# Attention's values by seven products, split between the recurrence and the projections, with ten pairs' first sums kept in DRAM

## The chip, the cores and the metric

The kernel runs on one core of one Trainium2 chip. That core has TensorE (PE in the profile; its weight loads are PEld), VectorE (DVE), ScalarE (ACT), GpSimd (POOL) and SyncE (SP, which issues most transfers). The metric is the device time in microseconds of one execution, and the time of a kernel is the median of its runs.

## The reference

One layer of an encoder on x of 1024 positions by 1024 features, all in float32. An input projection gives attention's q, k and v, the q, k, v and output gate of a gated linear attention (GLA), its decays, and two merge gates; then

```python
proj = x @ w_in[l]
(aq, ak, av, gq, gk, gv, gout, lr_f, lr_b, gate_a, gate_g) = jnp.split(proj, IN_SPLITS, axis=-1)
# mixer A: 12 heads of 64 in three groups (window, dilation) = (128,1), (512,4), (2048,16):
#   softmax over a dilated window with a position bias, o_g and its denominator per group
y_attn = jnp.sum(mix_w[..., None] * jnp.stack(outs, axis=0), axis=0)      # 4 heads x 64
# mixer B: chunked recurrence over chunks of 64, forward and backward, 4 heads
o_gla = o_fwd + o_bwd
y_gla = o_gla * lax.rsqrt(mean(o_gla**2) + eps) * gla_norm_g * silu(gout)
merged = sigmoid(gate_a) * (y_attn @ w_attn_branch) + sigmoid(gate_g) * (y_gla @ w_gla_branch)
x = _layernorm(ALPHA * x + merged @ w_out, ...)
x = _layernorm(ALPHA * x + square(relu(x @ w_ff1 + b_ff1)) @ w_ff2 + b_ff2, ...)
```

Attention's values `av`, which the change is about, are x (1024 x 1024) times a weight of 1024 x 768.

## The kernel before

**Arithmetic.** TensorE multiplies in a format of fewer bits than float32. Each operand is therefore split in two: a hi part, rounded by a cast on ACT, and a lo part, the operand less its hi part, by a subtraction on DVE (`halve`, `load_w`, `fm_pairs`). `mm3` makes each product as three matmuls: hi by hi (L102), hi by lo (L103), lo by hi (L104). The three lines carry nearly all matmuls of the kernel.

**Seven products.** A product of two matrices, each cut in 2 x 2 blocks, can be made of seven block products instead of eight, of sums of blocks (the Strassen-Winograd form). The kernel calls them m1 to m7, or M1 to M7. Their sides are A11, S1, S2, A12, S3, A22, S4 from the weights and B11, B21, T1 to T4, B22 from x. The T sums of x are made by `xsum` on DVE (L497) and split into `xT1` to `xT4`. A partial result that several blocks share (`cu`, the u2 of the form) is kept in SBUF; `cr` holds a result before SP stores it to the DRAM tensor `spill`.

**The order of the work.** The kernel is written in the order in which the engines get their work; each engine has its own queue and runs it in order, and `tc.issue_after` places an instruction behind a named earlier one in the scheduler's order. The stages are:

1. Start: the first blocks of GLA's q and k, then the decays and the values of GLA's first group (to 78.8 us, with the first heads' gating).
2. The recurrence (78.8 to 210.6 us). Each of four heads goes through `pre1`, `pre2`, `turn`, `intra`, `kv`, `states`, `out`, `outt`. Between these small steps stand big independent matmul units, the `fills`, taken by `fill(n)`: 8 units of GLA's values, 4 of its q and k, and 16 units of attention's V. A V unit is a token tile of 128 rows by 384 columns over all eight k-blocks, 24 matmuls, whose result ACT copies to `stgv` (L470) and SP stores to the DRAM tensor `vdr`. `extra` names for each fill by its number (`count`) what is done after it: loads and splits of later weights. Behind the last head's `out` the rest of the fills, three V units, stand ahead of `outt`.
3. The feature-major projections, in pairs of 128-row blocks (`proj`), by seven products, each of 12 matmuls of 512 columns (four k-blocks by three parts). The first two pairs (blocks 4 to 7, the GLA output gate) have M1 and M2 made together ahead of a list `steps`, which holds a preparation (a side) and a product each. Then come 14 pairs of seven steps: the q and k blocks of attention's groups 2, 1, 0 and eight pairs of merge gates.
4. Attention: 24 tiles (`att`), handled in 26 visits (`visit(i)`). A visit is a unit that runs ahead of a step, every 2.5 steps before the change: scores on PE, bias and maximum on DVE (L828), exponent on ACT (L834), transposes and the product with V in later visits. The loop over `steps` runs at step i the units named for i, then the preparation of step i + 3, and then the products of step i. The GLA output gating (`silu`, L979 and L980 on DVE) is among the units too.
5. Branches and merge, w_out, LayerNorm, the two feed-forward products (seven products each), LayerNorm. The change does not touch them.

TensorE's results go to PSUM tiles `mm`, `sc`, `tr`; `p_raw` (4 buffers) holds raw weights, `p_side` (7 buffers, named pwhi, pwlo, px after their pools) the split sides, and `p_sum` (psum) the running sum.

## Time and profile before

| | |
|---|---|
| median of 3 runs (lowest, highest) | 1370.29 us (1369.72, 1371.16) |
| the profiled execution's own time | 1370.95 us |
| its span, first to last instruction | 1368.5 us |
| mean granted TensorE clock | 0.998 |
| busy PE / PEld / DVE / ACT / POOL | 1357.7 / 1130.7 / 1008.9 / 630.5 / 113.6 us |
| moved by DMA | 241.75 MB, 177 GB/s on average |

All lines below are of one profiled execution. Busy time counts an engine's instructions without double counting of overlaps; matmuls overlap in the records, so a busy PE tells that something was in the pipeline, and the distance between starts tells how fast it ran. A row of windows gives, for one stretch of time, the busy microseconds of each engine with the number of its instructions in brackets, then the granted clock, the DMA share and the rate. A row of waits names the waiting instruction, an arrow, the instruction that released it, and the total, the number and the longest of the waits. A row of groups gives the line, the operation, output and inputs with their shape and count, the total and mean (ns) of one, and the idle time ahead of them on that engine with its cause.

### The profile page before, as it was taken

What the parts mean: (1) busy time and instruction counts of PE and PEld (TensorE: products, weight loads), DVE (VectorE), ACT (ScalarE), POOL (GpSimd) and SP (SyncE); (2) the same over time, 40 slices, a digit from 0 to 9 for tenths busy, and PEclk for the clock granted to TensorE, in tenths of its full rate; (3) what the DMA queues carried; (4) which work ended last, traced back from release to release, by engine and by line L of the source; (5) the groups of instructions that cost most, each with busy time, mean ns of one, the idle gap of its engine ahead of it and who ended that gap; (6) DMA issues with size and microseconds to landing.
All of it is one profiled execution on the core that took longest, in us unless ns stands there. A gap on an engine that the chain in (4) does not pass through costs nothing.

```text
span 1368.5 us, 18991 instructions
## 1 busy us (share of the span) xinstructions
PE 1357.7 (99%) x6829; PEld 1130.7 (83%) x6829; DVE 1008.9 (74%) x1748; ACT 630.5 (46%) x1207; POOL 113.6 (8%) x173
## 2 busy tenths in 40 slices
PE   9999999999999999999999999999999999999998
PEld 7989998877778777788888888888888888888886
DVE  7377767776566688767667778877867897786988
ACT  5346645334344444455326655555556433333343
POOL 0000100013333333100001000000000000000002
PEclk9999999999999999999999999999999999999999
DMA  8262326664554577665935465666645954445313
GB/s 254 67 200 80 104 75 193 207 189 142 162 172 140 154 214 173 202 229 194 339 127 197 160 223 199 215 206 211 244 178 176 372 204 156 154 142 162 97 31 123
DMA packets 119234, 241.75 MB, mean 177 GB/s; under 512 B 33269, under 2 KB 42133, under 8 KB 119140
## 3 DMA queue, kind: packets, MB, share of 16 engines
q1 hardware_dynamic: 111764, 220.57, 48.7%
q0 software_dynamic: 6944, 19.54, 5.0%
q8 instruction: 53, 0.87, 0.3%
q10 hardware_dynamic: 432, 0.44, 0.1%
q14 instruction: 41, 0.34, 0.1%
HBM read 163.81 MB, written 77.73 MB: 177 GB/s over the span
## 4 chain that ended last, share of the span: by engine, by line
PE 88%; DVE 5%; DMA 3%; ACT 2%; issue 1%; POOL 0%; SPq 0%; ACTq 0%; DVEq 0%; POOLq 0%
PE ps L102 18%; PE ps L103 18%; PE ps L104 18%; PE mm L102 8%; PE mm L103 8%; PE mm L104 8%; PE sc L822 1%; PE avp L861 1%; PE tr L846 1%; DMA pwhi<-in_wfm 1%; DVE cr L654 1%; ACT xr L1261 1%; PE sc L409 0%; DMA xr<-in_xT 0%; PE tr L379 0%
## 5 line engine op out<-in xcount | busy, mean ns | idle before, releaser
L1242 ACT CAST T<-hp 128x1024 fp32r<-128x1024 f32 x36 | 37.9, 1052 | 110.7 <-PE ps L103 71.0
L103 PE MATMUL mm<-wlo,x 128*128 128x272 f32 (+1 forms) x240 | 74.5, 311 | 0.7 <-DVE wlo L95 0.7
L102 PE MATMUL mm<-whi,x 128*128 128x272 f32 (+1 forms) x240 | 75.0, 313 | 0.0
L104 PE MATMUL mm<-whi,x 128*128 128x272 f32 (+1 forms) x240 | 74.7, 311 | 0.0
L103 PE MATMUL ps<-B,B 128*128 128x512 f32 x160 | 62.2, 389 | 0.0
L104 PE MATMUL ps<-B,B 128*128 128x512 f32 x160 | 62.2, 389 | 0.0
L102 PE MATMUL ps<-B,B 128*128 128x512 f32 x160 | 60.9, 390 | 0.5 <-ACT B L1242 0.5
L1748 POOL TENSOR_TENSOR mv<-mv,mhalf 128x1 f32<-128x1 f32 x8 | 7.0, 880 | 607.3 <-DVE mv L1747 605.8
L834 ACT ACTIVATE e<-e,sm 128x256 f32<-128x256 f32 (+2 forms) x96 | 43.4, 453 | 30.0 <-DVE sm L828 29.9
L102 PE MATMUL ps<-T,T 128*128 128x512 f32 x144 | 56.0, 389 | 0.0
L103 PE MATMUL ps<-T,T 128*128 128x512 f32 x144 | 56.0, 389 | 0.0
L104 PE MATMUL ps<-T,T 128*128 128x512 f32 x144 | 56.0, 389 | 0.0
L102 PE MATMUL ps<-B,T 128*128 128x512 f32 x144 | 56.0, 389 | 0.0
L103 PE MATMUL ps<-B,T 128*128 128x512 f32 x144 | 56.0, 389 | 0.0
L104 PE MATMUL ps<-B,T 128*128 128x512 f32 x144 | 56.0, 389 | 0.0
L1243 DVE TENSOR_TENSOR T<-hp,T 128x1024 fp32r<-128x1024 f32 x36 | 43.9, 1221 | 15.5 <-ACT T L1242 15.4
L1643 DVE TENSOR_TENSOR acc<-ps,acc 128x512 f32<-128x512 f32 x68 | 45.5, 685 | 12.8 <-PE ps L104 12.3
L102 PE MATMUL mm<-x,pwlo 128*128 128x512 f32 x128 | 50.7, 396 | 0.7 <-ACT cu L659 0.7
L654 DVE TENSOR_TENSOR cr<-cu,mm 128x512 f32<-128x512 f32 x44 | 35.2, 800 | 20.3 <-PE mm L104 20.1
L102 PE MATMUL ps<-T,fraw 128*128 128x512 f32 x128 | 49.6, 390 | 0.4 <-ACT T L1242 0.4
L104 PE MATMUL mm<-x,pwlo 128*128 128x512 f32 x128 | 49.9, 390 | 0.0
L103 PE MATMUL mm<-x,pwlo 128*128 128x512 f32 x128 | 49.9, 389 | 0.0
(492 smaller groups left out, 4197.2 us busy)
## 6 DMA issues: line engine op xcount, KB each, us to landing
hdr<-c SPq DMA_DIRECT2D x112, 256.0 KB, 3.0
hp<-hdr SPq DMA_DIRECT2D x56, 512.0 KB, 3.9
spill<-cr SPq DMA_DIRECT2D x64, 256.0 KB, 2.9
praw<-in_wfm SPq DMA_DIRECT2D x16, 512.0 KB, 5.3
pwhi<-in_wfm SPq DMA_DIRECT2D x16, 512.0 KB, 4.6
gate<-spill SPq DMA_DIRECT2D x32, 256.0 KB, 3.1
wa<-in_w SPq DMA_DIRECT2D x16, 512.0 KB, 4.4
wb<-in_w SPq DMA_DIRECT2D x16, 512.0 KB, 7.2
```

Source lines behind the costliest of these rows:

```text
L102: T.matmul(ps, lh, rh, start=first and i == 0, stop=False, skip_group_check=more)
L103: T.matmul(ps, lh, rl, start=False, stop=False, skip_group_check=more)
L104: issued["pe"] = T.matmul(ps, ll, rh, start=False, stop=last and i == n - 1, skip_group_check=more)
L654: issued["add"] = V.tensor_tensor(o, a, b, op=OP.add)
L822: mm = T.matmul(sps[i][:, pr, 0:w], q[ps_, pr], k[ps_, pr, 0:w], start=True, stop=True)
L834: issued["exp"] = A.activation(e, e, AF.Exp, bias=sm[:, h:h + 1], scale=-1.0, accum_out=sm[:, 4 + h:5 + h])
L846: T.transpose(tp[0:hi - lo, pr, j], b["e"][i][:, pr, lo:hi], ident)
L861: return T.matmul(av[64 * i:64 * i + 64, pr], vv[:, h * 64:h * 64 + 64], b["et"][i][p0:p0 + vv.shape[0], pr, j], start=j == pr == 0, stop= ...
L1242: A.copy(o[:, 0], src)
L1243: V.tensor_tensor(o[:, 1], src, o[:, 0].bitcast(F32), op=OP.subtract)
L1261: A.activation(q[i][:, k], tp[:, k], AF.Identity, bias=cols[:, c + 8:c + 9], scale=cols[:, c:c + 1])
L1643: V.tensor_tensor(m, p, m, op=OP.add)
```

## The change

V is made by seven products too. Its 1024 x 768 weight is cut into 2 x 2 blocks of 512 x 384, x likewise. M1 and M2 of V are made for four token tiles in the recurrence (`att_v`, `part`): M1's sum is stored in a DRAM tensor `vpk`, M1 + M2 in `vdr`. The other five products of V are ten half-steps (`v_prep`, `v_do`, with two of the four k-blocks each) in `steps`, behind the first two pairs and ahead of the rest. `v_fetch` loads raw V weights into `p_raw`, `v_kept` reads `vpk` back into attention's R tiles `vu`, and the sums go into attention's av and ak tiles `vx`.

Ten of the 14 later pairs (`KEPT`) make M1 and M2 in the recurrence as well (`first_two`): raw weights are loaded and split, M1 is copied by ACT and stored to a DRAM tensor `upk`, and M1 + M2 to `spill`. Their `proj` then has five steps in place of seven; the first of them (`sums`) reads `upk` back into `cu` and prepares S1 and S2. The fills of the recurrence become 12 + 14 in place of 28; each of the 14 (`two`) holds two half units of 12 matmuls each, of 512 columns for a pair and 384 for V, in the order of `halves`, so that M1 of the next stands between M1 and M2 of one. One fill in place of three stands behind the last head's `out`.

The list `steps` has 98 entries in place of 108, visits come at fixed steps (`at`), and the gating units come earlier in time beside the V half-steps, in other buffers. The core of the diff:

```diff
-    def att_v(c):
-        w, raws, order = {}, [], (0, 1, 2, 3) if c == 0 else (3, 0, 1, 2)
+    todo = [((4, 5), 1), ((6, 7), 1)]
+    for g in (2, 1, 0):
+        todo += [((b + 2 * g, b + 2 * g + 1), ORD[g]) for b in (24, 30)]
+    todo += [((b, b + 1), 1) for b in range(8, 24, 2)]
+    NP = len(todo)
+    KEPT = 10
+
+    def after_raw(f, *a):
+        with tc.issue_after(issued["raw"].ins):
+            return f(*a)
+
+    def keep(dst, ps, r=1):
+        n = ps.shape[1]
+        o = xb_t() if n == 512 else stg.tile([128, n], F32, tag="stgv", bufs=2, name="stgv")
+        o = o.rearrange("p (c j) -> p c j", c=r)
+        A.copy(o, ps.rearrange("p (j c) -> p c j", c=r))
+        SP.dma_start(dst, o if r > 1 else o[:, 0])
+
+    def first_two(p):
+        (b0, _), r = todo[2 + p]
+        st = {}
+
+        def fetch_raw():
+            st["raw"] = wp.tile([128, KT, 128], F32, tag="raw", bufs=2, name="raw")
+            issued["raw"] = after_raw(SP.dma_start, st["raw"], io["wfm"][b0])
+
+        def split():
+            st["w"] = fm_pairs(*load_w(None, [128, KT, 128], st["raw"]), 0)
+
+        def m1():
+            st["ps"] = mmtile()
+            mm3(st["ps"], st["w"][0:4])
+            keep(upk[p], st["ps"])
+
+        def m2():
+            mm3(st["ps"], st["w"][4:8], False, True, True)
+            keep(spill[b0].rearrange("p (c h j) -> p h c j", h=2, c=r)[:, 0] if r > 1 else spill[b0][:, 0:512], st["ps"], r)
+        return fetch_raw, split, m1, m2
+
+    def att_v():
...
+        def part(t, h):
             ts = slice(t * 128, t * 128 + 128)
-            mm3(ps, [(xh(k, ts), xl(k, ts), w[k // 2][0][:, k % 2], w[k // 2][1][:, k % 2])
-                     for i in order for k in (2 * i, 2 * i + 1)])
-            o = stg.tile([128, 384], F32, tag="stgv", bufs=2, name="stgv")
-            A.copy(o, ps)
-            SP.dma_start(vdr[ts, c * 384:c * 384 + 384], o)
-        return fetch_raw, split, [lambda t=t: unit(t) for t in range(8)]
+            if h == 0:
+                ps[t] = mmtile(384)
+            mm3(ps[t], [(xh(k, ts), xl(k, ts), w[k // 2][0][:, k % 2], w[k // 2][1][:, k % 2])
+                        for k in range(4 * h, 4 * h + 4)], h == 0, True, h == 1)
+            keep(vdr[ts, 0:384] if h else vpk[t], ps[t])
...
-    (_, split0, v0), (raw1, split1, v1) = att_v(0), att_v(1)
+    v_raw, v_split, v_parts = att_v()
+    firsts = [first_two(p) for p in range(KEPT)]
+    halves = [f[2:] for f in firsts] + v_parts
+    halves = [halves[0][0]] + [f for a, b in zip(halves, halves[1:]) for f in (b[0], a[1])] + [halves[-1][1]]
     gv_load, fills = gla_v_units(1)
     gv_load()
-    fills += q_units + k_units + v0 + v1
-    extra = {1: [q_load, k_load], 9: [lambda: split0(0), lambda: split0(1)], 10: [lambda: split0(2)],
-             11: [lambda: split0(3)], 13: [lambda: raw1(0), lambda: raw1(1)],
-             14: [lambda: raw1(2), lambda: raw1(3)],
-             17: [lambda: split1(3)], 19: [lambda i=i: split1(i) for i in range(3)]}
...
+    def two(n):
+        if 0 < n <= 12:
+            after_raw(SP.dma_start, tdr[n - 1], trow[n - 1:n].to_broadcast([128, 512]))
+        step(halves[2 * n])
+        step(halves[2 * n + 1])
+    fills += q_units + k_units + [lambda n=n: two(n) for n in range(len(halves) // 2)]
+    extra = {1: [q_load, k_load]}
+    for p in range(KEPT):
+        extra.setdefault(8 + p, []).append(firsts[p][0])
+        extra.setdefault(9 + p, []).insert(0, firsts[p][1])
+    for n, f, i in ((13, v_raw, 0), (13, v_raw, 1), (14, v_raw, 2), (14, v_raw, 3),
+                    (17, v_split, 3), (19, v_split, 0), (20, v_split, 1), (21, v_split, 2)):
+        extra.setdefault(n, []).append(lambda f=f, i=i: f(i))
...
+        def sums():
+            c["u2"] = cu()
+            with behind("sp"):
+                issued["sp"] = SP.dma_start(c["u2"], upk[kept])
+            s1()
+            s2()
+        if kept is not None:
+            return dict(raw=raw, steps=[(sums, [m6]), (side("S3"), [m7]), (lambda: None, [m5]), (side("A22"), [m4]),
+                                        (side("S4"), [m3])])
...
+    def v_prep(n, u):
+        o = vs[:, u]
+        with behind("add"):
+            if n == 5:
+                V.tensor_tensor(o, vraw[1, 0, u], vraw[1, 1, u], op=OP.add)
+            elif n == 6:
+                V.tensor_tensor(o, o, vraw[0, 0, u], op=OP.subtract)
+                V.tensor_tensor(vraw[1, 0, u], vraw[0, 0, u], vraw[1, 0, u], op=OP.subtract)
+            elif n == 3:
+                V.tensor_tensor(o, vraw[0, 1, u], o, op=OP.subtract)
+        vside[n, u] = hi, lo = [p_side().rearrange("p a b -> p (a b)")[:, 0:768] for _ in range(2)]
+        halve(hi, lo, {7: vraw.get((1, 0, u)), 4: vraw.get((1, 1, u))}.get(n, o))
+        for k in {(5, 0): ((0, 0, 0), (1, 0, 0)), (5, 1): ((0, 0, 1), (1, 0, 1)), (6, 0): ((1, 1, 0),),
+                  (7, 0): ((1, 1, 1),), (7, 1): ((0, 1, 0), (0, 1, 1))}.get((n, u), ()):
+            v_fetch(*k)
+        if (n, u) in ((4, 1), (3, 1)):
+            projs[2 if n == 4 else 3]["raw"]()
...
+    def v_do(n, u):
+        hi, lo = (x.rearrange("p (k f) -> p k f", k=2) for x in vside[n, u])
+        nm = {5: "T1", 6: "T2", 7: "T3", 4: "T4", 3: "B22"}[n]
+        for t in range(4):
+            ts = slice(t * 128, t * 128 + 128)
+            if u == 0:
+                vps[n, t] = vps[7, t] if n == 4 else banks_of[0]()[:, 0:384]
+            ps = vps[n, t]
+            fresh = u == 0 and n != 4
+            mm3(ps, [(xside(nm, 0, 2 * u + j)[:, ts], xside(nm, 1, 2 * u + j)[:, ts], hi[:, j], lo[:, j])
+                     for j in range(2)], fresh, u == 1, n == 4)
+            if u == 0:
+                continue
+            if n == 5:
+                A.copy(vx[t], ps)
+                continue
+            o = {6: vu[t], 4: vu[t], 3: vx[t]}[n] if n != 7 else cr()[:, 0:384]
+            add(o, vx[t] if n == 7 else o, ps)
+            if n == 6:
+                add(vx[t], vx[t], o)
+                continue
+            r, c = {7: (4, 1), 4: (0, 1), 3: (4, 0)}[n]
+            with behind("sp"):
+                issued["sp"] = SP.dma_start(vdr[(r + t) * 128:(r + t) * 128 + 128, c * 384:c * 384 + 384], o)
...
-    n0 = len(steps) + 14
+    units = {}
+    units[4] = [lambda: v_fetch(1, 0, 0), lambda: v_fetch(1, 1, 0)]
+    units[6] = [v_kept]
+    units[7] = [lambda: v_fetch(1, 0, 1), lambda: v_fetch(1, 1, 1)]
+    for i, (n, u) in enumerate((n, u) for n in (5, 6, 7, 4, 3) for u in range(2)):
+        units.setdefault(8 + i, []).append(lambda n=n, u=u: v_prep(n, u))
+        steps.append((lambda: None, [lambda n=n, u=u: v_do(n, u)]))
+    n0 = len(steps) + 10
+    units.setdefault(18, []).append(projs[2]["steps"][0][0])
+    projs[2]["steps"][0] = (lambda: None, projs[2]["steps"][0][1])
     for p in projs[2:]:
         steps += p["steps"]
     n1 = len(steps) - 7
-    units = {}
+    at = [2 * min(i, 8) + 1.75 * min(max(i - 8, 0), 8) for i in range(26)]
     for i in range(26):
-        n = n0 + 5 + i * (n1 - 6 - n0) // 25
+        n = n0 + 5 + int(at[i] + max(i - 16, 0) * (n1 - 6 - n0 - at[-1]) / 9)
...
-        n = n0 - 18 + i * 3 // 2
-        for n, f in zip((n, n + 5), silu(i // 2, i % 2)):
+        for n, f in zip((8 + 2 * i, 12 + 2 * i), silu(i // 2, i % 2)):
```

What this makes of the queues is shown at three places.

DVE at the end of the recurrence, before: `xT1k` are the splits of the first T sum, `on` scales the last head's output, `xraw` (L497) are sums of x's blocks.

```order
L152 TENSOR_TENSOR xT10_1969<-xraw0_327,xT10_1969 128x512
L152 TENSOR_TENSOR xT11_1973<-xraw1_328,xT11_1973 128x512
L152 TENSOR_TENSOR xT12_1977<-xraw2_329,xT12_1977 128x512
L152 TENSOR_TENSOR xT13_1981<-xraw3_330,xT13_1981 128x512
L428 TENSOR_TENSOR on_1941<-av_1932,ss_1942 128x512
L428 TENSOR_TENSOR on_1959<-tr_1950,ss_1960 128x512
L497 TENSOR_TENSOR xraw0_327<-xb220_331,xraw0_327 128x512
L497 TENSOR_TENSOR xraw1_328<-xb221_332,xraw1_328 128x512
```

And after, at the same place (line numbers are those of the changed kernel; L154 is the split, L430 the scaling, L530 the sums of x):

```order
L154 TENSOR_TENSOR xT10_2028<-xraw0_329,xT10_2028 128x512
L154 TENSOR_TENSOR xT11_2032<-xraw1_330,xT11_2032 128x512
L154 TENSOR_TENSOR xT12_2036<-xraw2_331,xT12_2036 128x512
L154 TENSOR_TENSOR xT13_2040<-xraw3_332,xT13_2040 128x512
L154 TENSOR_TENSOR pwlo_2123<-pwhi_2118,pwlo_2123 128x512
L154 TENSOR_TENSOR pwlo_2124<-pwhi_2118,pwlo_2124 128x512
L154 TENSOR_TENSOR pwhi_2120<-praw_2126,pwhi_2120 128x512
L430 TENSOR_TENSOR on_2000<-av_1991,ss_2001 128x512
L430 TENSOR_TENSOR on_2018<-tr_2009,ss_2019 128x512
L530 TENSOR_TENSOR xraw0_329<-xb222_335,xraw0_329 128x512
L530 TENSOR_TENSOR xraw1_330<-xb220_333,xraw1_330 128x512
```

Three splits of the first pairs' weights (pwlo, pwhi) now stand ahead of the two `on` rows; the rest keeps its order.

PE at the end of the four products M1, M1, M2, M2 of the first two pairs, before: mm_2126 is M5 (S1 by T1) of the first pair and mm_2124 that of the second; a tile of p_side (here pwhi) holds a side's hi and lo part, and of the three lines only L104 reads the lo part.

```order
L102 MATMUL mm_2125<-x10_93,pwlo_2120 128x512
L103 MATMUL mm_2125<-x10_93,pwlo_2120 128x512
L104 MATMUL mm_2125<-x10_93,pwlo_2120 128x512
L102 MATMUL mm_2126<-xT10_1969,pwhi_2117 128x512
L103 MATMUL mm_2126<-xT10_1969,pwhi_2117 128x512
L102 MATMUL mm_2124<-xT10_1969,pwhi_2116 128x512
L103 MATMUL mm_2124<-xT10_1969,pwhi_2116 128x512
L104 MATMUL mm_2126<-xT10_1969,pwhi_2117 128x512
L102 MATMUL mm_2126<-xT11_1973,pwhi_2117 128x512
L103 MATMUL mm_2126<-xT11_1973,pwhi_2117 128x512
L104 MATMUL mm_2126<-xT11_1973,pwhi_2117 128x512
```

After, where sc_2131 is M7 (S3, in px, by T3):

```order
L102 MATMUL mm_2129<-x10_95,pwlo_2124 128x512
L103 MATMUL mm_2129<-x10_95,pwlo_2124 128x512
L104 MATMUL mm_2129<-x10_95,pwlo_2124 128x512
L102 MATMUL mm_2130<-xT10_2028,pwhi_2121 128x512
L103 MATMUL mm_2130<-xT10_2028,pwhi_2121 128x512
L102 MATMUL mm_2128<-xT10_2028,pwhi_2120 128x512
L103 MATMUL mm_2128<-xT10_2028,pwhi_2120 128x512
L102 MATMUL sc_2131<-xT30_2090,px_2117 128x512
L103 MATMUL sc_2131<-xT30_2090,px_2117 128x512
L104 MATMUL mm_2130<-xT10_2028,pwhi_2121 128x512
L102 MATMUL mm_2130<-xT11_2032,pwhi_2121 128x512
L103 MATMUL mm_2130<-xT11_2032,pwhi_2121 128x512
L104 MATMUL mm_2130<-xT11_2032,pwhi_2121 128x512
```

The two products' first matmuls are now followed by two of a third one before the first lo part is read, and mm_2128 goes on later.

DVE where the steps of the first two pairs end, before: results are added from PSUM (L654) and the next pair's sides prepared (L639, L641, L152, 512 columns).

```order
L654 TENSOR_TENSOR cr1_2108<-cr1_2108,mm_2124 128x512
L639 TENSOR_TENSOR psum0_2111<-praw_2123 128x512
L152 TENSOR_TENSOR pwlo_2119<-psum0_2111,pwlo_2119 128x512
L641 TENSOR_TENSOR psum0_2111<-psum0_2111,praw_2122 128x512
L654 TENSOR_TENSOR cr2_2109<-cu1_2106,tr_2130 128x512
L152 TENSOR_TENSOR pwhi_2116<-psum0_2111,pwhi_2116 128x512
L152 TENSOR_TENSOR pwlo_2118<-pwhi_2114,pwlo_2118 128x512
L152 TENSOR_TENSOR pwlo_2121<-praw_2123,pwlo_2121 128x512
L654 TENSOR_TENSOR cr3_2110<-cu1_2106,mm_2124 128x512
L647 TENSOR_TENSOR praw_2123<-praw_2122,praw_2123 128x512
L979 TENSOR_TENSOR et0_2259<-et0_2259,e0_2255 128x512
```

After, V's half-steps begin here: L633 adds from PSUM, L1049 to L1052 are sums of V's raw weights, L154 splits, both of 768 columns, and L1025 and L1026 the gating.

```order
L633 TENSOR_TENSOR cr1_2112<-cu1_2110,tr_2134 128x512
L633 TENSOR_TENSOR cr1_2112<-cr1_2112,mm_2128 128x512
L1049 TENSOR_TENSOR vs_2281<-praw_2126,praw_2127 128x768
L154 TENSOR_TENSOR pwlo_2123<-vs_2281,pwlo_2122 128x768
L633 TENSOR_TENSOR cr2_2113<-cu1_2110,tr_2134 128x512
L1049 TENSOR_TENSOR vs_2281<-pwhi_2118,pwhi_2119 128x768
L633 TENSOR_TENSOR cr3_2114<-cu1_2110,mm_2128 128x512
L1025 TENSOR_TENSOR e1_2260<-e1_2260,e0_2259 128x512
L154 TENSOR_TENSOR pwlo_2124<-vs_2281,pwhi_2120 128x768
L1051 TENSOR_TENSOR vs_2281<-vs_2281,praw_2126 128x768
L1026 TENSOR_TENSOR e1_2260<-e1_2260,et0_2263 128x512
L1052 TENSOR_TENSOR praw_2127<-praw_2126,praw_2127 128x768
```

V's first sums and splits stand between the additions of the first pairs; on DVE's queue nothing separates them.

More of the change, by code (lines that the diff above doesn't have):

```diff
@@ L456, in split @@
             else:
-                w[i] = load_w(io["wtv"][c, i], [128, 2, 384], raws[i] if raws else None)
-        def unit(t):
-            r = c * 8 + t - 2
-            if 0 <= r < 12:
-                with tc.issue_after(issued["raw"].ins):
-                    SP.dma_start(tdr[r], trow[r:r + 1].to_broadcast([128, 512]))
-            ps = mmtile(384)
-            ts = slice(t * 128, t * 128 + 128)
-            mm3(ps, [(xh(k, ts), xl(k, ts), w[k // 2][0][:, k % 2], w[k // 2][1][:, k % 2])
-                     for i in order for k in (2 * i, 2 * i + 1)])
-            o = stg.tile([128, 384], F32, tag="stgv", bufs=2, name="stgv")
-            A.copy(o, ps)
-            SP.dma_start(vdr[ts, c * 384:c * 384 + 384], o)
-        return fetch_raw, split, [lambda t=t: unit(t) for t in range(8)]
+                w[i] = load_w(None, [128, 2, 384], raws[i])
+        def part(t, h):
+            ts = slice(t * 128, t * 128 + 128)
+            if h == 0:
[3 more added lines that the diff above has]
+            keep(vdr[ts, 0:384] if h else vpk[t], ps[t])
+        return fetch_raw, split, [[lambda t=t, h=h: part(t, h) for h in range(2)] for t in range(4)]
     xraw = {}
@@ L518, in build @@
     heads = [gla_head(h) for h in range(4)]
-    def after_raw(f, *a):
-        with tc.issue_after(issued["raw"].ins):
-            f(*a)
     def step(f, *a):
@@ L589, in build, with add, proj @@
     banks_of = [turns(mm_t + more_t, 7), turns(mm_t[1:] + mm_t[:1], 3)]
+    def add(o, a, b):
+        issued["add"] = V.tensor_tensor(o, a, b, op=OP.add)
     def behind(k):
         return tc.issue_after(issued[k].ins) if k in issued else nullcontext()
-    def proj(blocks, r, ahead, banks):
+    def proj(blocks, r, ahead, banks, kept=None):
         st, c, ps = {}, {}, {}
@@ L970, in load @@
         def load():
-            b["g"], b["y"], b["s"] = (n() for n in gating)
+            b["g"], b["y"], b["s"] = gating()
             SP.dma_start(b["g"], spill[4 + h, :, sl])
@@ new lines, in v_kept @@
+    def v_kept():
+        for t in range(4):
+            with behind("sp"):
+                issued["sp"] = SP.dma_start(vu[t], vpk[t])
+    def v_prep(n, u):
[15 more added lines that the diff above has]
+            projs[2 if n == 4 else 3]["raw"]()
@@ new lines, in v_do @@
+    def v_do(n, u):
+        hi, lo = (x.rearrange("p (k f) -> p k f", k=2) for x in vside[n, u])
+        nm = {5: "T1", 6: "T2", 7: "T3", 4: "T4", 3: "B22"}[n]
+        for t in range(4):
+            ts = slice(t * 128, t * 128 + 128)
[16 more added lines that the diff above has]
+            r, c = {7: (4, 1), 4: (0, 1), 3: (4, 0)}[n]
+            with behind("sp"):
+                issued["sp"] = SP.dma_start(vdr[(r + t) * 128:(r + t) * 128 + 128, c * 384:c * 384 + 384], o)
```

36 lines of the change are left out of this document (19 added, 17 removed).

## The prediction

> **What bounds the kernel now.** I read the page's busy shares and chain first, then the windows of the stages that the change touches, then what TensorE (PE) waits for in them, and only then single durations.
>
> ```profile
> span 1368.5 us, 18991 instructions
> PE 1357.7 (99%) x6829; PEld 1130.7 (83%) x6829; DVE 1008.9 (74%) x1748; ACT 630.5 (46%) x1207; POOL 113.6 (8%) x173
> PE 88%; DVE 5%; DMA 3%; ACT 2%; issue 1%; POOL 0%; SPq 0%; ACTq 0%; DVEq 0%; POOLq 0%
> ...
> 78.79:210.58 131.79, 131.11 (x872) 123.32 (x871) 95.49 (x146) 72.64 (x176) 9.86 (x14) 1.00 0.41 128
> 210.58:301.86 91.28, 90.33 (x399) 74.18 (x398) 66.24 (x102) 36.07 (x61) 3.64 (x5) 1.00 0.64 195
> 301.86:386.79 84.93, 84.75 (x469) 67.35 (x470) 54.41 (x148) 36.49 (x113) 27.78 (x42) 1.00 0.51 162
> 386.79:463.26 76.47, 76.47 (x466) 60.80 (x464) 46.76 (x122) 33.01 (x94) 25.68 (x37) 1.00 0.48 154
> 463.26:587.16 123.90, 121.78 (x698) 96.65 (x697) 98.32 (x297) 55.18 (x144) 32.62 (x50) 1.00 0.68 194
> ```
>
> The windows are the recurrence with its fills, the first projections up to the first attention visit, and the attention's groups 2, 1 and 0; the columns are length, busy PE, weight loads, DVE, ACT, POOL, clock, DMA share, GB/s. PE is busy in nearly all of each, at full clock. Does "busy" mean work, though? Recorded matmuls overlap, so I look at their starts: first and last of 47 matmuls of a V projection, and of 26 of 512 columns.
>
> ```profile
> 134.07 0.34 PE L103 MATMUL mm<-wlo,x 128*128 128x384 f32 x1
> ...
> 142.04 0.34 PE L104 MATMUL mm<-whi,x 128*128 128x384 f32 x1
> ...
> 234.26 0.39 PE L102 MATMUL tr<-xT,pwlo 128*128 128x512 f32 x1
> ...
> 239.93 0.39 PE L102 MATMUL mm<-x,pwlo 128*128 128x512 f32 x1
> ```
>
> That is 7.97/46 = 0.173 us for 384 columns and 5.67/25 = 0.227 for 512: evenly spaced, and in the ratio 0.76 against 0.75 for the columns. PE is bound by the columns it streams, so a removed matmul is worth its pitch, provided nothing else stops PE. What stops it between 78 and 590 us is little:
>
> ```profile
> PE sc L928 <- DVE sm L828: 1.2, 3, 0.6
> PE mm L102 <- ACT cr L679: 0.9, 1, 0.9
> PE mm L102 <- ACT cu L659: 0.7, 1, 0.7
> PE mm L103 <- DVE wlo L95: 0.7, 2, 0.4
> ```
>
> (total, times, longest). The Trainium skill, in "Perfetto Trace Analysis", section "Identifying the Most-Contended Engine", says that matmul occupancy is a poor measure of headroom and that the busy share of weight loads is a good one. By it the 83% of PEld would leave 17% unused; the even starts above speak against it, and it comes back below as a rival.
>
> **The change, part by part.**
>
> *Removed matmuls.* V before is 16 units of 8 k-blocks by 3, 384 matmuls of 384 columns; as seven products over 4 token tiles, 4 k-blocks and 3 parts it is 7 x 48 = 336. 48 x 0.173 = **8.3 us saved**. Nothing else leaves or joins PE: the ten pairs' M1 and M2 are the same 24 matmuls of 512 columns each (5.44 us a pair), made earlier.
>
> *Moved matmuls.* Recurrence: 16 V units (16 x 24 x 0.173 = 66.6 us) go, 20 half units of 12 x 0.227 and 8 V halves of 12 x 0.173 come, 54.4 + 16.6 = 71.0; behind it stands a V block of 240 x 0.173 = 41.6 us; the attention loses 54.4. The moves cancel: 71.0 + 41.6 - 54.4 - 66.6 = -8.4, the saving above.
>
> *Recurrence's side work.*
>
> ```profile
> L1243 DVE TENSOR_TENSOR T<-hp,T 128x1024 fp32r<-128x1024 f32 x36 | 43.9, 1221 | 15.5 <-ACT T L1242 15.4
> L1242 ACT CAST T<-hp 128x1024 fp32r<-128x1024 f32 x36 | 37.9, 1052 | 110.7 <-PE ps L103 71.0
> L659 ACT COPY cu<-mm 128x512 f32<-128x512 f32 x15 | 8.7, 582 | 4.8 <-PE mm L104 4.8
> L470 ACT COPY stgv<-mm 128x384 f32<-128x384 f32 x16 | 7.5, 471 | 21.0 <-PE mm L104 21.0
> ```
>
> A kept pair's weights are split there, 1024 columns (1.22 on DVE, 1.05 on ACT), and its two results are copied out by ACT (0.58 each); of V's splits (0.955 and 0.838, below) 4 of 8 go, of its copies (0.471) 8 of 16. DVE gains 12.2 - 3.8 = 8.4, ACT 10.5 + 11.6 - 7.1 = 15.0, in a stage that grows by 4.4 to 136.2 us: DVE 76%, ACT 64%. Transfers gain 7.3 MB (raw weights and kept sums 5.2 each, V's first sums 0.8, less 1.6 of V weights and 2.4 of V results) on 16.9: 178 GB/s, which the next stage already exceeds with 195. The cover of all this is the fills: a result's copy of 0.58 stands beside the next product's 2.7 us before M2 is added to the same bank. Of the old waits, the 0.7 on cu was M1's copy in the first of the ten pairs and goes with it; the 0.7 on wlo is of V's splits, two of which now come at other fills, so I take half: **-1.1**. New waits on the ten splits: between 0 and 3.5 (0.35, the old mean of two, each time); in fills two ahead, nearer nothing, **+0.5**.
>
> *The first pairs' sums behind the recurrence.* Here cover is lost. Three V units (12.5 us) stood between the last head's outputs and the first pair's M1; one fill of 4.16 is left, so M1 to the T products come 8.3 us earlier against DVE's queue. That queue is full:
>
> ```profile
> 200.05 0.69 DVE L428 TENSOR_TENSOR on<-tr,ss 128x512 f32<-128x512 f32 x1 [1.09 <-POOL ss L427]
> 200.66 3.69 DVE L497 TENSOR_TENSOR xraw<-xb,xraw 128x512 f32<-128x512 f32 x6
> 204.27 2.49 DVE L152 TENSOR_TENSOR xT<-xraw,xT 128x512 fp32r<-128x512 f32 x4
> ...
> 224.24 0.68 DVE L152 TENSOR_TENSOR pwlo<-psum,pwlo 128x512 fp32r<-128x512 f32 x1
> 228.32 0.69 DVE L152 TENSOR_TENSOR pwlo<-psum,pwlo 128x512 fp32r<-128x512 f32 x1 [3.40 <-ACT pwlo L151]
> 200.66:224.93 24.27, 24.27 (x125) 21.79 (x124) 23.89 (x40) 17.34 (x31) 0.00 (x0) 1.00 0.53 163
> ...
> 221.57 0.39 PE L102 MATMUL mm<-xT,pwhi 128*128 128x512 f32 x1
> ```
>
> Six operations start 0.602 apart (204.27 - 200.66 = 3.61), and DVE is busy 23.89 of 24.27. Counted against the recurrence's end, the first T product moves from 221.57 to 213.3. In the changed order DVE's splits of the first blocks stand ahead of the last `on`; S1's lo of the first pair is the 21st operation behind it and ends at 200.66 + 21 x 0.602 = 213.3, where PE wants it six matmuls into the products, 214.6; the second pair's is the 25th, 215.7 against 16 matmuls, 216.9. Margins of 1.2 us. Bounds: 0, and 8.3 if DVE's finishing times don't move at all; the count is nearest to nothing, but a landing such as the 0.33 us that DVE waited here before eats a quarter of the margin: **+0.5**. "VectorE: DVE Perf Modes" of the Trainium skill, section "The DRAIN you can't avoid", has the next held operation start only when the pipe has emptied; at 0.69 from start to start the 25th would end at 217.9 and the wait be 1.0 instead of 0.5. The row with 0.602 disagrees for these operations.
>
> *The V block.* Durations:
>
> ```profile
> L95 DVE TENSOR_TENSOR wlo<-xraw,whi 128x768 fp32r<-128x768 f32 x3 | 2.8, 955 | 0.0
> L874 DVE COPY R<-avp 128x256 f32<-128x256 f32 x16 | 6.7, 420 | 0.8 <-PE avp L861 0.8
> L654 DVE TENSOR_TENSOR cu<-cu,mm 128x512 f32<-128x512 f32 x13 | 8.9, 686 | 14.6 <-PE mm L104 14.6
> L979 DVE TENSOR_TENSOR et<-et,e 128x512 f32<-128x512 f32 x5 | 3.4, 689 | 0.0
> L93 ACT CAST whi<-xraw 128x768 fp32r<-128x768 f32 x3 | 2.5, 838 | 1.1 <-PE mm L104 1.1
> praw<-in_wfm SPq DMA_DIRECT2D x10, 512.0 KB, 4.8
> ```
>
> 18 sums and splits x 0.955 = 17.2; 20 adds of 384 from PSUM, between 0.420 (256 columns) and 0.686 (512), the middle 0.553: 11.1; four gatings of two, 5.5; the next pair's first two sides, 4.1. That is 37.9 of 41.6 us by durations (91%), less by starts. Sides are prepared two half-steps (8.3 us) ahead, and a raw block of 512 KB lands in 4.8. Bounds: 0, and 3 if the block's first side, queued behind the adds of the first pairs, is late by one chain of sum, cast and split (0.955 + 0.838 + 0.955 = 2.7); the count has it just in time, **+0.5**. DMA moves 13 to 15 MB here, some 260 GB/s in 58 us, where the page's slices reach 372: hidden.
>
> *The attention.* A kept pair takes 5.44 us of PE away and two halves of DVE (1.4). Groups 2 and 1: PE 161.4 - 6 x 5.44 = 128.8, DVE 101.2 - 8.3 = 92.9, a load of 72%, where group 0 already runs at 98.32/123.90 = 79% and PE idles 2.1 us. Visits come every two and then 1.75 steps instead of 2.54. Bounds: 0, and 4 (16 visits by a quarter us, between the three waits on sm and none); **+0.5**, nearer nothing because of the 79%.
>
> *Hidden.* The kept sums' reload (`upk`, ten of 256 KB by SP) comes three steps (8 us) ahead of the addition that reads it; it is late only if SP's queue is held by an output store for longer than that less a landing (4.8 for twice the bytes). The later silu timing moves DVE work of equal size. Both at nothing.
>
> **Sum.** The profiled execution took 1370.95, 0.66 above the median of 1370.29: 1370.95 - 8.3 - 1.1 + 2.0 = 1363.5, and against the median **1362.9**.
>
> **Rivals.** A measurement of this kernel can tell about 0.2%, 2.7 us, from no change.
>
> 1. *The first pairs' sums are late.* If DVE's work can't move up (a side's hi waits for ACT, a block of x lands late), 4 to 8.3 us come back: 1366.5 to 1370.7, typically 1368. For it: 98% busy; against: the count of 21 and 25. 10%.
>
> 2. *DVE stalls in order in the V block.* Each half-step casts on ACT before DVE can subtract; if DVE stands through the whole 0.838 instead of finding other work, it needs 3.79 + 0.84 = 4.63 a half-step against PE's 4.16, +4.7 over ten: 1367.1; with adds at 0.8 as well, +10, 1372. For it: 91% already; against: sides are made two half-steps ahead. 10%.
>
> 3. *The attention becomes bound by its own chain (slower).* With less product work between visits, scores, exp and transposes of one visit are not done when the next starts. At 0.9 us (the longest wait of the list above) on each of 16 visits, +14.4 - 0.5: 1376.8. It is slower than before from 0.8 us a visit. For it: two visits are one step apart. Against: group 0. 8%.
>
> 4. *PE isn't the bound* (the skill's rule above): starts would be set by something that does not shrink with columns, and the 48 matmuls return nothing: 1370 to 1371. The 0.76 ratio speaks against it. 3%.
>
> The forecast holds 69%, 1359.5 to 1366: the lower end is every new wait at nothing (1360.9) and the three waits on sm gone too. Faster takes the forecast, half of rival 1 and most of rival 2: 0.78; the rest of both and rival 4 give the same, 0.13; rival 3 and a bad rival 2, slower, 0.09. For 8 in 10 the range reaches to 1370.
>
> **What would show it.** Right: PE's busy time down by some 8 us, the recurrence some 4.4 longer, a V block near 42 us, groups 2 and 1 some 33 shorter, and no line of PE's waits over 1 us there. Wrong: waits of T products on DVE's pwlo or pwhi (1), of 384-column products on DVE or DMA (2), of scores or transposes on sm, e or et above 8 us (3), or a longer pitch (4).

## The result, and the profile after

The changed kernel takes 1375.76 us (median of 12 runs, 1372.63 to 1381.11) where the kernel before takes 1370.55 in the same sessions (1369.29 to 1371.75): 1.0041 of it, 95% interval 1.0029 to 1.0053. It is slower by 5.2 us. The forecast, 1362.9 within 1359.5 to 1370.0, was wrong in size and in sign. The runs of the changed kernel also lie 8.5 us apart, against 2.5 before.

The profiled execution is the quickest of the twelve (1372.63), so what it shows is less than the typical loss. From its page, then the windows of its stages: the recurrence with the first M1 and M2 (before: 142.78 us), the first pairs' products, the V block, and the stretch from the V block to the first scores.

```profile
span 1370.8 us, 18987 instructions
PE 1352.6 (99%) x6781; PEld 1124.4 (82%) x6781; DVE 1029.1 (75%) x1772; ACT 632.5 (46%) x1199; POOL 113.4 (8%) x173
PE 90%; DVE 3%; DMA 2%; issue 2%; ACT 2%; POOL 1%; SPq 0%; ACTq 0%; POOLq 0%; DVEq 0%
...
78.79:225.79 147.00, 146.56 (x873) 127.52 (x872) 108.59 (x160) 91.27 (x205) 9.60 (x14) 1.00 0.55 172
225.79:254.09 28.30, 27.52 (x121) 22.41 (x120) 20.55 (x33) 8.72 (x13) 0.00 (x0) 1.00 0.54 167
254.09:295.86 41.77, 41.77 (x241) 41.60 (x240) 34.08 (x51) 13.72 (x21) 0.00 (x0) 1.00 0.84 287
295.86:341.86 46.00, 39.58 (x157) 31.27 (x157) 30.26 (x44) 9.63 (x16) 3.64 (x5) 0.93 0.58 171
```

The page's busy share is no help: 99%, and 5 us less busy time than before. The last window is where to look. PE is idle there for 6.4 us, and the granted clock is 0.93, where it is full in the other three. What PE waits for over the whole run:

```profile
PE mm L102 <- DVE cr L633: 6.3, 2, 3.6
PE sc L871 <- DMA ak<-spill: 1.5, 1, 1.5
PE mm L102 <- ACT cr L720: 1.4, 1, 1.4
...
PE tr L102 <- DVE cr L633: 0.8, 1, 0.8
PE sc L977 <- DVE sm L877: 0.7, 2, 0.5
```

Two waits on the addition that writes cr (L633) make 6.3 us. In the timeline of PE both stand ahead of a product M4:

```profile
303.83 0.39 PE L104 MATMUL mm<-xT,pwlo 128*128 128x512 f32 x1
306.99 0.79 PE L102 MATMUL mm<-xT,pwhi 128*128 128x512 f32 x1 [2.77 <-DVE cr L633]
307.58 0.63 PE L103 MATMUL mm<-xT,pwhi 128*128 128x512 f32 x1
...
322.30 0.39 PE L104 MATMUL mm<-xT,pwlo 128*128 128x512 f32 x1
326.25 0.50 PE L102 MATMUL mm<-xT,pwlo 128*128 128x512 f32 x1 [3.57 <-DVE cr L633]
327.56 0.63 PE L104 MATMUL mm<-xT,pwlo 128*128 128x512 f32 x1
```

The recorded 0.63 us in place of 0.39 is the slow clock behind a wait. Two windows, during the first wait and behind it:

```profile
304.00:306.90 2.90, 0.22 (x1) 0.00 (x0) 2.24 (x4) 1.15 (x3) 0.00 (x0) 1.00 0.30 90
307.30:310.40 3.10, 3.10 (x8) 2.43 (x8) 3.10 (x6) 0.62 (x1) 0.00 (x0) 0.50 0.41 112
```

So each of these two waits is paid with a second bill: some eight matmuls at 0.427 us in place of 0.227, 1.6 us. The last section shows what sets it.

A balance by starts. From each matmul's distance to the next I take the median distance of its shape in the kernel before; the medians sum to the pure streaming time, the rest is lost time.

```
                    streaming   lost
before              1353.24     9.14
after               1344.94    20.96
                     -8.30    +11.82
```

The saving is there as forecast, 8.3. It is more than eaten by 11.8 us of lost time: the last matmul starts 3.5 us later, and the span is 2.3 longer, since what lies behind that matmul was 1.2 shorter in this execution. Between V block and first scores 156 matmuls of 0.2268 us (35.4) took 46.0, so 10.6 of the 20.96 us are lost in this stretch alone.

**Why M4 waits.** M4 is summed into the bank that holds M7, so DVE must first have added M7 to u2 (the addition to cr), and that needs u2 + M6 (the addition to cu, which holds u2). In the code M5 stands between M7 and M4 and covers this. In TensorE's printed order it doesn't. At the second kept pair (mm_2130 holds M7, then M4; mm_2129 is M6, mm_2128 is M5) these are the first row of each run of rows of one product:

```
L102 MATMUL mm_2130<-xT30_2090,px_2117 128x512        M7 (T3)
L102 MATMUL mm_2129<-xT20_2211,pwlo_2125 128x512      M6 (T2), two matmuls only
L102 MATMUL mm_2128<-xT10_2028,pwhi_2121 128x512      M5 (T1)
L104 MATMUL mm_2129<-xT20_2211,pwlo_2125 128x512      M6, the other ten
L102 MATMUL mm_2130<-xT4_2105,pwlo_2122 128x512       M4 (T4)
```

M6 ends just ahead of M4, and the whole chain of sums stands open. In the first kept pair the order is M5, M6, M7, M4. DVE at the second wait, whose columns are start, length, line, operation and idle time before:

```profile
322.72 0.69 DVE L633 TENSOR_TENSOR cu<-cu,mm 128x512 f32<-128x512 f32 x1 [5.78 <-PE mm L104]
323.33 0.68 DVE L1025 TENSOR_TENSOR e<-e,e 128x512 f32<-128x512 f32 x1
323.93 0.69 DVE L688 TENSOR_TENSOR psum<-pwhi,psum 128x512 f32<-128x512 f32 x1
324.53 0.69 DVE L154 TENSOR_TENSOR pwlo<-praw,pwlo 128x512 fp32r<-128x512 f32 x1
325.13 1.06 DVE L633 TENSOR_TENSOR cr<-cu,mm 128x512 f32<-128x512 f32 x1
```

DVE had stood idle for 5.8 us until M6 was done; then three operations that M4 doesn't need (a gating product, a sum, a split) stand ahead of the one it does need.

### The profile page after: what moved, and what is told of

It reads as the page before. It is cut to its first block, busy times and chain, and to the rows that moved or that the text cites. A ratio compares the mean times of both kernels' runs of the same rounds, so it can differ in the third digit from the quotient of the medians.

```text
span 1370.8 us, 18987 instructions
## 1 busy us (share of the span) xinstructions
PE 1352.6 (99%) x6781; PEld 1124.4 (82%) x6781; DVE 1029.1 (75%) x1772; ACT 632.5 (46%) x1199; POOL 113.4 (8%) x173
## 4 chain that ended last, share of the span: by engine, by line
PE 90%; DVE 3%; DMA 2%; issue 2%; ACT 2%; POOL 1%; SPq 0%; ACTq 0%; POOLq 0%; DVEq 0%
PE ps L102 18%; PE ps L103 18%; PE ps L104 18%; PE mm L102 8%; PE mm L104 8%; PE mm L103 8%; PE sc L871 1%; PE tr L895 1%; PE avp L910 1%; PE sc L102 1%; PE sc L104 1%; PE sc L103 1%; ACT xr L1372 1%; DVE cr L633 0%; PE tr L102 0%
## 5 line engine op out<-in xcount | busy, mean ns | idle before, releaser
L104 PE MATMUL ps<-B,B 128*128 128x512 f32 x160 | 62.3, 389 | 0.0
L104 PE MATMUL ps<-B,T 128*128 128x512 f32 x144 | 56.1, 390 | 0.0
L104 PE MATMUL ps<-T,T 128*128 128x512 f32 x144 | 56.1, 389 | 0.0
L1354 DVE TENSOR_TENSOR T<-hp,T 128x1024 fp32r<-128x1024 f32 x36 | 44.0, 1222 | 15.3 <-ACT T L1353 13.6
L102 PE MATMUL mm<-x,whi 128*128 128x512 f32 x136 | 53.6, 404 | 0.5 <-ACT xb L460 0.4
L102 PE MATMUL mm<-xT,pwlo 128*128 128x512 f32 x120 | 48.8, 407 | 5.0 <-DVE cr L633 3.6
L103 PE MATMUL mm<-x,whi 128*128 128x512 f32 x136 | 53.7, 395 | 0.0
L104 PE MATMUL mm<-x,wlo 128*128 128x512 f32 x136 | 53.4, 394 | 0.0
L633 DVE TENSOR_TENSOR cr<-cu,mm 128x512 f32<-128x512 f32 x44 | 35.1, 798 | 20.6 <-PE mm L104 20.3
L102 PE MATMUL ps<-T,fraw 128*128 128x512 f32 x128 | 49.7, 390 | 0.4 <-ACT T L1353 0.4
L103 PE MATMUL ps<-T,fraw 128*128 128x512 f32 x128 | 49.9, 390 | 0.0
L104 PE MATMUL ps<-T,fraw 128*128 128x512 f32 x128 | 49.7, 390 | 0.0
```

Source lines behind the costliest of these rows:

```text
L102: T.matmul(ps, lh, rh, start=first and i == 0, stop=False, skip_group_check=more)
L103: T.matmul(ps, lh, rl, start=False, stop=False, skip_group_check=more)
L104: issued["pe"] = T.matmul(ps, ll, rh, start=False, stop=last and i == n - 1, skip_group_check=more)
L633: issued["add"] = V.tensor_tensor(o, a, b, op=OP.add)
L1354: V.tensor_tensor(o[:, 1], src, o[:, 0].bitcast(F32), op=OP.subtract)
```

## The experiments

All are edits of the changed kernel, timed beside the kernel before; ratios are to it. Theories A and B were put against each other first, in four kernels.

**The products' order forced.**

```diff
-            with behind("small"):
+            with behind("prod" if kept is not None and "prod" in issued else "small"):
                 mm3(ps[b], [...], not more, True, more)
+            if kept is not None:
+                issued["prod"] = issued["pe"]
```

> The changed kernel with one addition: each product of a kept pair is placed behind the last matmul of the product before it, so that M5 stands between M7 and M4 on TensorE in all ten pairs (in the changed kernel M4 follows M7 directly in the first kept pair and M6 in the second). Theory A, the products' order: M4 accumulates on the bank that DVE must first have read, and with nothing between them TensorE waits for the whole chain of additions. Then the waits of 2.9 and 3.7 us on DVE's cr go, the slow clock behind them (about 3 us of added pitch) goes too: 1362.5 to 1364.5, granted clock 0.998, and the runs lie within 2.5 us of each other as those of before do. Theory B, the gating's loads and stores hold the queues of SP and ACT, whatever the order: the waits move to the next product that needs a split or a stored sum, 1370 or more, and the spread of 8 us stays.

Measured: 1370.50, ratio 1.0002 (0.9992 to 1.0012). The wait of the second kept pair is gone with its slow clock, 5.3 us of the median. The runs draw together, ten of eleven within 3.4 us. But the 1362.5 to 1364.5 of theory A were not reached: at the first kept pair, now in the order M6, M7, M5, M4, PE still waits for 3.04 us. One row each of PE, DVE, ACT and SP around it tells why:

```profile
307.56 0.50 PE L102 MATMUL mm<-xT,pwhi 128*128 128x512 f32 x1 [3.04 <-DVE cr L633]
...
300.32 0.69 DVE L154 TENSOR_TENSOR pwlo<-pwhi,pwlo 128x512 fp32r<-128x512 f32 x1
305.83 0.69 DVE L154 TENSOR_TENSOR pwlo<-psum,pwlo 128x512 fp32r<-128x512 f32 x1 [4.82 <-ACT pwlo L153]
306.44 1.06 DVE L633 TENSOR_TENSOR cr<-cu,mm 128x512 f32<-128x512 f32 x1
...
304.66 0.63 ACT L1025 ACTIVATE et<-e 128x512 f32<-128x512 f32 x1 [5.15 <-DMA e<-spill]
305.20 0.60 ACT L153 CAST pwlo<-psum 128x512 fp32r<-128x512 f32 x1
...
297.96 0.32 SPq L1021 DMA_DIRECT2D e<-yodr  x1
300.95 0.39 SPq L1020 DMA_DIRECT2D e<-spill  x1
...
SPq L1021 <- DMA ygdr<-e: 11.5, 4, 3.5
```

Read it from the bottom. SP may issue the gating's load of y only when the store of the unit two before it has landed, since there are two sets of buffers (four such waits, 11.5 us). Everything behind it in SP's queue is late, so the gate's load goes out at 300.95. ACT's sigmoid waits for it until 304.66, and the cast behind the sigmoid is done at 305.8. DVE stands 4.82 us before that cast's split, and the addition that M4 needs stands behind the split. Four queues in order, and one late load stops TensorE.

**The visits spread as well.**

```diff
-    at = [2 * min(i, 8) + 1.75 * min(max(i - 8, 0), 8) for i in range(26)]
+    at = [2 * min(i, 16) for i in range(26)]
```

> As order_forced, and the first 16 visits of the attention come every two steps, with no gap of one step. Theory A expects 1361 to 1363, 1.7 us below order_forced, by the one wait of scores on the load of ak (1.5 us) that the changed kernel has where two visits are one step apart. Theory B: 1368 or more. If the visits' spacing is no cause, the time is that of order_forced.

Measured: 1373.33, ratio 1.0016 (1.0007 to 1.0025), 2.8 above order_forced. The expectation failed: order_forced has no wait on ak left to take away, and the two steps of room given to group 1 are missing in group 0. There the waits grew from 3.3 to 6.2 us in all. The largest of PE's waits from 459 us on, here and then in order_forced:

```profile
PE sc L979 <- DVE sm L879: 2.9, 4, 1.7
PE mm L102 <- DVE cr L633: 1.9, 2, 1.0
PE sc L979 <- DVE f L973: 0.9, 2, 0.7
```

```profile
PE sc L979 <- DVE sm L879: 1.6, 2, 0.9
PE mm L102 <- ACT cr L722: 1.1, 1, 1.1
PE mm L102 <- DVE cr L633: 0.6, 1, 0.6
```

**The gating left out.**

```diff
-            g, y, sg = b["g"], b["y"], b["s"]
-            A.activation(sg, g, AF.Sigmoid)
-            ... the two multiplications on DVE
-            SP.dma_start(ygdr[h, :, sl], y)
+            SP.dma_start(ygdr[h, :, sl], b["y"])
```

> The changed kernel without the output gating's activation and two multiplications (ygdr gets yodr as it is; the eight loads of a gate and of y and the eight stores stay). The products' order becomes better in the second kept pair (M5 ahead of M4) and stays bad in the first (M4 behind M7). Theory A: the wait of 3.7 us goes, that of 2.9 shrinks to the one addition of 1.06 to 1.2 us that M4 must wait for: 1365 to 1367. Theory B: ACT and DVE have nothing more to wait for, no wait over 0.5 us is left there, 1362 to 1364.

Measured: 1369.19, ratio 0.9984 (0.9974 to 0.9993). In its trace M4 of the first kept pair waits for 1.25 us (306.94), the one addition, and the 3.7 us are gone: both as theory A put it. The time is 2 us above A's range, by waits that A didn't name (1.6 us at 353.11, and 2.2 at 447.78 on ak). Leaving the gating's work out is worth 6.6 us in a stage where it was to be free, but not all of it is the gating's. Without it the compiled order is another: in the second kept pair M5 (from 317.93) now stands ahead of M4 (321.11), so this kernel has a part of the forced order too.

**The gating's transfers by POOL.**

```diff
-            SP.dma_start(b["g"], spill[4 + h, :, sl])
-            SP.dma_start(b["y"], yodr[h, :, sl])
+            G.dma_start(b["g"], spill[4 + h, :, sl])
+            G.dma_start(b["y"], yodr[h, :, sl])
...
-            SP.dma_start(ygdr[h, :, sl], y)
+            G.dma_start(ygdr[h, :, sl], y)
```

> The changed kernel with the gating's loads and stores issued by POOL in place of SP; TensorE's order of products is that of the changed kernel. Theory A: the wait of 3.7 us at the second kept pair stays (M6, its addition, a split and the second addition stand between), the one of 2.9 us shrinks to between 1.1 and 2.9: 1370 to 1375. Theory B: SP issues the reload of upk and the raw weights at once, both waits go: 1362 to 1365.

Measured: 1374.14, ratio 1.0025 (1.0012 to 1.0037). The wait at the second kept pair stays (3.57 us), that at the first falls to 1.63. Both waits and the time are what theory A forecast here; theory B's forecast failed. The time alone can't be told from that of the changed kernel, whose interval was 1.0029 to 1.0053. The profiled execution is the quickest of the ten, and no slow clock follows the 3.57 us in it; the other nine have a lower mean clock (0.994 to 0.998, here 0.999). With order_forced, where the first wait stayed, the two runs say that the order makes the second wait, and that SP's queue makes a part of the first. So neither theory is the whole of it. That is theory C of the next runs.

**Order and POOL together.** The two edits at once.

> The products' order forced as in order_forced, and the gating's loads and stores issued by POOL as in gating_by_pool. order_forced still has one wait of 3.0 us at the first kept pair: DVE stands 4.82 us for a cast that ACT has behind a sigmoid, which waits for the gate's load, which SP issued late because a load of y ahead of it waited for an earlier store. Theory C, both causes hold, each at its own pair (order at the second, SP's queue by way of ACT at the first): with both mended no wait over 1 us is left between 290 and 345 us, and the time falls by that 3.0 plus 1.5 of slow clock from order_forced's 1370.5: 1365 to 1367, runs within 3 us. Theory A alone (order only) expects 1370 as for order_forced. Theory D, the projections are short of DVE here whoever issues the loads: the wait moves to the next product, 1369 to 1371.

Measured: 1365.65, ratio 0.9957 (0.9945 to 0.9970), faster than both kernels and within theory C's 1365 to 1367; between 290 and 345 us the longest wait left is 0.2. The stretch that was lost now runs at full clock, here as windows of order_and_pool and then of the changed kernel:

```profile
290.00:345.00 55.00, 54.82 (x259) 44.99 (x258) 45.39 (x74) 17.02 (x32) 12.09 (x21) 1.00 0.73 230
```

```profile
290.00:345.00 55.00, 48.58 (x210) 39.72 (x209) 38.69 (x66) 13.03 (x22) 3.64 (x5) 0.94 0.63 191
```

The same 55 us hold 49 more instructions of PE. The medians of the four form a square: 1375.76 as changed, 1370.50 with the order (-5.3), 1374.14 with POOL (-1.6), 1365.65 with both (-10.1). Together they give 3.2 us more than the two apart. That is at the edge of what these runs can tell, since each of the four ratios is known to some 1.4 to 1.8 us either way, and why it should be so is not shown. The lost time from the V block's end to the first scores shows the same in the traces (length, less matmuls times 0.2268):

```
after                 46.00 - 156 x 0.2268 = 10.6
gating_by_pool        43.18 - 156 x 0.2268 =  7.8
order_forced          43.27 - 168 x 0.2268 =  5.2
order_and_pool        39.10 - 168 x 0.2268 =  1.0
order_three_buffers   38.30 - 168 x 0.2268 =  0.2
```

The 7.8 of gating_by_pool has no second bill behind its wait of 3.57; with one, as most of its runs seem to have, it would be some 9.4.

**Order, and three sets of buffers, SP as issuer.**

```diff
-    gating = turns([[flat(x) for x in y] for y in (es_[0:2] + ets[0:1], es_[2:4] + ets[1:2])], 2)
+    gating = turns([[flat(x) for x in y] for y in (es_[0:2], es_[2:4], ets[0:2])], 3)
+    sig = turns([flat(x) for x in (ets[2], aks[1])], 2)
```

> The products' order forced, and the gating's buffers in three sets for gate and y (two for the sigmoid) in place of two sets; SP issues as before. If the two sets are what holds SP (its load of y waits for the store of the unit two before to land, five times, 11.4 us in all), the load of the gate comes early, ACT doesn't wait, and the time is that of order_and_pool, 1365 to 1367. If SP's queue is held by the stores of V's results and of the pairs (which wait for DVE), three sets change little: 1369 to 1371.

Measured: 1366.07, ratio 0.9960 (0.9947 to 0.9972), the same as with POOL. So it is not SP as such: two sets of buffers, whose release waits for a store to land, held its queue.

> Order forced, three sets of buffers, and POOL as issuer: Theory C expects no more than the better of the two others, 1364.5 to 1367; if loads by POOL are themselves the limit (each holds POOL some 0.7 us and lands no sooner), 1367 to 1370.

Order, three sets and POOL: 1366.09, ratio 0.9962 (0.9949 to 0.9976). So the two ways of mending the queue win no more together than either alone.

**Where do the last 2 to 3 us stand?** order_and_pool is 2.8 above the forecast; against the kernel before in its own session (1371.32) it saves 5.7 us where 7.4 were forecast. Two kernels tried the attention's last group.

```diff
+    WHICH = [2, 3, 4, 5, 6, 7, 12, 13, 14, 15]
-        (b0, _), r = todo[2 + p]
+        (b0, _), r = todo[WHICH[p]]
...
-                          i - 2 if 1 < i < 2 + KEPT else None))
+                          WHICH.index(i) if i in WHICH else None))
```

> order_and_pool, but the ten kept pairs are the six of attention's q and k and the last four of the merge gates, in place of the first four, so that group 0 of the attention runs beside pairs of seven products. order_and_pool still loses some 3.7 us of TensorE's time between 480 and 600 us, mostly waits of scores on DVE's sm. Theory E, a kept pair leaves DVE more work for each step of products, and group 0 is where DVE is fullest: the waits on sm fall from 1.3 to under 0.6 us and the time to 1363.5 to 1365. If the waits come from the visits themselves, whatever stands beside them: 1365 to 1366.5. If the last four pairs, beside the branches' splits, lose as much as is won: 1366 to 1369, with new waits behind 560 us.

Measured: 1380.46, ratio 1.0076 (1.0063 to 1.0088): 14.8 us worse than order_and_pool, the third of the expected cases and far beyond its size. PE's waits in it:

```profile
PE mm L102 <- DVE cr L634: 8.5, 2, 4.6
PE mm L102 <- ACT pwhi L153: 4.3, 1, 4.3
PE avp L913 <- DVE W L934: 2.2, 1, 2.2
...
PE sc L980 <- DVE sm L880: 0.7, 2, 0.4
```

The waits on sm did fall, from 1.3 to 0.7, as theory E had it. But kept pairs beside the last visits and their combination work wait for sides and sums instead. A kept pair has five splits, four sums of weights and five additions for five products (13.6 us of PE); a whole pair has seven, four and five for seven (19.1 us). Per microsecond of PE a kept pair asks more of DVE. Yet DVE isn't short of time here: from 460 to 600 us it is busy for 98.80 us, in order_and_pool for 108.59. It stands, for a load of the combination's weights W from the DRAM tensor fdr, here and then in order_and_pool, both from 460 to 600 us:

```profile
DVE W L934 <- DMA W<-fdr: 18.3, 5, 6.1
```

```profile
DVE W L933 <- DMA W<-fdr: 8.6, 5, 3.3
```

Two of PE's three longest waits (3.85 us at 554.05, 4.63 at 580.70) come behind such a stand of 1.37 and 2.51 us: the products of W follow it, and the addition that PE needs stands behind them in DVE's queue. That is the first kept pair's story once more, with another load. No run took the load away, so how much of the 14.8 us it makes stays open.

```diff
-    at = [2 * min(i, 8) + 1.75 * min(max(i - 8, 0), 8) for i in range(26)]
+    at = [2 * min(i, 8) + 1.5 * min(max(i - 8, 0), 8) for i in range(26)]
```

> order_and_pool with the visits of group 1 every 1.5 steps in place of 1.75, which leaves group 0 three per cent of a step more each (3.0 in place of 2.78). Tighter spacing in group 0 cost 2.8 us in order_and_visits against order_forced. If that scales, the waits on sm go and group 1 pays: 1364.5 to 1366.5; a gain of more than 1 us (under 1364.7) would say that group 0 alone is short of time, a loss of more than 1 us (over 1366.7) that group 1 with visits one step apart is now.

Measured: 1368.02, ratio 0.9980 (0.9970 to 0.9990), 2.4 above order_and_pool in the median, though four of the nine runs (1365.65 to 1367.06) lie within order_and_pool's (1362.77 to 1368.38). The expectation reads such a loss as group 1 being short of room, and that doesn't follow: the edit did not reach group 1. In TensorE's order the scores of the first 19 visits stand behind the same number of products as in order_and_pool; only those of the 20th and 21st, both of group 0, came one product earlier. A wait of 2.18 us on sm at 495.09, at the 20th visit, with the slow clock behind it, makes most of the difference in the profiled execution, which is the slowest of the nine. Whether more room for group 0 would help was not tested. Which waits make up the last 2.8 us was not tried further; in order_and_pool's trace the largest are 1.35 and 1.04 us at 573.43 and 482.77, and 0.94 and 0.60 at 248.45 and 145.94.

## Why the prediction was wrong

- *What bounds the kernel, and the removed matmuls*: right. 48 matmuls fewer, 8.30 us less streaming time; the evenly spaced starts carried the argument, and the rival that PE isn't the bound is out.
- *Recurrence*: right. 147.00 us up to the first T product against 142.78, +4.2 where 4.4 was forecast; the wait on cu (0.7) and the two on wlo (0.7) went, where -1.1 was put for them, and the new splits cost no wait. A wait of 0.44 us on ACT's copy of a kept sum is new.
- *The first pairs' sums* (rival 1): right, no wait at the T products; 0.8 us later on one result (248.5) against 0.5 forecast. The prediction sets its row with 0.602 against the section "The DRAIN you can't avoid" of "VectorE: DVE Perf Modes" in the Trainium skill. That section of the Trainium skill lets a next operation that is not held start earlier. Nothing here shows that those six operations were held, so the row doesn't speak against it.
- *The V block* (rival 2): right. 41.77 us for 41.6, DVE 34.08 of it (82%), not one wait over 0.2. The addition of 384 columns from PSUM was put at 0.553 and measured 0.55:

```profile
293.22 0.55 DVE L633 TENSOR_TENSOR av<-av,tr 128x384 f32<-128x384 f32 x1
```

- *The attention* (rival 3): 0.5 forecast; the profiled execution has 1.5 on ak (0.3 before) and 0.7 on sm (1.2 before), so 0.7 more on the two: near the forecast.
- *"The later silu timing moves DVE work of equal size. Both at nothing"*: this is one of the two steps that failed. The work is of equal size, but for gate and y it went from six sets of buffers to two. Its last product starts at 326.7 us where the kernel before had it at 281.6 (so the gating ends later, and doesn't come earlier as the section on the change has it), and half of the units now stand beside pairs that have five products. Its transfers and its sigmoid stand in the same in-order queues as the casts that those products need. I priced the gating by its DVE time alone; what it costs is its place in SP's and ACT's queues. With the order forced, freeing SP's queue was worth 4.9 us (1370.50 to 1365.65). The other sentence there, on the reload of `upk`, held: DVE's additions to cu waited for PE (3.60 and 5.78 us at the two waits), never for that load. What SP's queue held up was the load of the gate.
- *No term at all* stood for the stretch between the V block and the first scores. This is the other step that failed, and the larger one alone: 5.3 us of the median went with the order forced. I took the products there in the order of the code, M5 between M7 and M4. The printed order has M4 behind M7 in one pair and behind M6 in the next, and I had read that order at three other places. With it the wait could have been bounded: two additions with a gating product, a sum and a split between them, 0.686 + 0.689 + 0.686 + 0.689 + 0.816 = 3.6 us by the rows of before. The second wait is 3.57.
- *The second bill*: every wait was priced at its length. One that leaves TensorE idle for most of a clock window costs 1.4 to 1.9 us more (last section).

With both steps mended 10.1 of the 12.9 us between forecast and measurement came back. Which waits hold the rest is open.

The typical run is 3.1 us above the profiled one. No trace shows the others; their granted clocks say that they were throttled for longer, 0.997 in the four quickest and 0.992 to 0.994 in the four slowest. A window of 3.41 us at half the clock is 0.00125 of 1370 us, so by an estimate from these means the slowest run had four slow windows more than the profiled one, which is 6.8 of the 8.5 us between them. With the order forced the clock is 0.996 or more in ten of eleven runs. That the lengths of the waits vary by when transfers land fits this, and is not shown.

## What to carry to other kernels

A saving on the bounding engine is only as good as the cover of the pieces that are left: where a product is taken out of a chain, read in the printed order, not in the code, what now stands between a product and the sum it must wait for. Price moved side work by every queue that it enters, transfers and activations too: one load that waits for a buffer can stop four engines one behind the other. And mend such waits together before judging either, since alone they were worth 5.3 us and 1.6 (no more than noise), together 10.1. Read in TensorE's order, too, whether an edit did what it was to do: one of those above did not.
